# A pass that orders the finished instruction list of an encoder layer by due times

## The chip, the cores and the metric

The kernel runs on one core of a Trainium2 chip. A core has a matrix engine (TensorE, "PE" in the profile; its weight loads are "PEld"), a vector engine (VectorE, "DVE"), a scalar engine (ScalarE, "ACT"), a general engine (GpSimd, "POOL") and a sync engine (SyncE, "SP"). Here SP issues all the transfers between the chip's main memory (HBM) and the on-chip memory (SBUF). Each engine works through its own list of instructions in order and waits for the others by semaphores. Results of TensorE go to eight PSUM banks, from which VectorE and ScalarE take them.

The metric is the device time of one execution in microseconds (us); less is better.

## The reference

One layer over 2048 tokens of width 1024, in float32, and a final normalisation:

```python
xn = rms_norm(x, mix_norm_g)
aq, ak, av, mq, mk, mv, mo, ipre, fpre, ga, gm = split(xn @ w_in)
att = chunk_band_attention(aq, ak, av, rel_bias)      # 8 heads of 64, chunks of 64, own + 8 before
q, k = silu(causal_depthwise_conv(concat(mq, mk)))    # width 4
hm = mlstm_chunkwise(q, k, mv, ipre + b_igate, fpre + b_fgate)   # 4 heads of 128
mlstm_out = sigmoid(mo) * rms_norm_by_head(hm)
y = sigmoid(ga) * (att @ w_att_proj) + sigmoid(gm) * (mlstm_out @ w_mlstm_proj)
x = x + y @ w_out
x = x + square(relu(rms_norm(x, ffn_norm_g) @ w_up)) @ w_down    # 4096 wide
return rms_norm(x, final_norm_g)
```

## The kernel before

The 2048 tokens are four blocks of 512 (`b` 0 to 3), two blocks make a span (`s` 0 and 1). Activations lie with features on the partitions and tokens along the free axis, so most matmuls move 512 columns.

**Two halves of each number.** Products are to have float32 accuracy. A float32 operand is split into a rounded part (type fp32r) and the rest. ScalarE makes the rounded part (`copy`), VectorE the rest (`tensor_sub`), and three matmuls are summed: high x high, high x low, low x high (`mm3`, lines 496 to 498). A weight tile of 128 x 1024 is loaded by SP into one of four buffers `wraw`, then split into one of three buffers `wsp` (`split_now`: line 435 on ScalarE, line 437 on VectorE). Activations are split in `split` (lines 1032 to 1039) into `r` tiles.

**Quads.** The large products use a two-by-two block scheme with seven products in place of eight (`quad`, line 579, and `quad_tok`, line 607). Sums of weight blocks are built either on the fly from four raw tiles (`quad_w`, line 454), or ahead of time by `sum_w` (line 404), which loads blocks into `ctx` tiles, adds them on VectorE and stores them in HBM (`wsum`). The four bank results of a quad are put together by `combine`: ScalarE copies the first product of a pair (line 1678), VectorE adds the second (line 1686), and the bank is free. Among the quads are both halves of the gate `ga` in both spans: `GATES` lists ga0, ga1, gm0, gm1 for span 0, and `IN_ORDER` has them for span 1. `down` adds the products of w_down into accumulators (line 2082), `after_out` those of w_out (line 1900).

**Chains beside the dense work.** Attention goes head by head: scores (line 1227) are reduced against the bias (1233), exponentiated on ScalarE (1242), scaled by the reciprocal of their sum (1244, 1246), transposed on PE (1258), split (1261, 1263) and multiplied with the values (1196). The mLSTM goes head by head in four chunks: transposed keys are scaled (1494, 1498), then three matmuls per chunk (1519 to 1521), and the state `cst` is updated on VectorE (1524) before the next chunk. Outputs of both (`mix`) go to HBM and are loaded back for the projections (`take_u1`, lines 2000 and 1032).

**What sets the order.** Python generators, one per strand of work, ask for buffers, banks and engine time; `Flow` runs them against its own clock of each engine and so writes all instructions in one list. Chain matmuls are put `SLACK` = 800 ns behind the moment at which `Flow` thinks they are ready. Buffers and banks are fixed at this point. The framework's scheduler then takes this list in order of priority, and on each engine brings an instruction forward where it finds it ready before earlier ones, by its own estimates. For example the memset of `hist` (line 317), written behind the loading of the gate weights, runs 0.86 us after the start. So the order on the engines is the scheduler's, with the list as its priority.

The last step of the program's build is in `Layer.build`:

```python
fl.spawn(self.late(), 0)
fl.spawn(self.dense(), 5)
fl.run()
```

Of the kernel before, what the change touches and what calls it, by code (L numbers as in the profile page):

```python
# [15 lines left out]


# [1 line left out]

# [49 lines left out]
class Event:  # L69
    def __init__(self):  # L70
        self.at = None
# [23 lines left out]
class Flow:  # L95
# [22 lines left out]
    def set(self, ev):  # L118
        ev.at = self.now
# [53 lines left out]
    def run(self):  # L173
        while self.ready or self.blocked:
            moved = True
            while moved:
                moved = False
                for th in sorted(self.blocked, key=lambda x: (x.prio, x.n)):
                    ok, value = self._grant(th)
                    if ok:  # L180
                        self.blocked.remove(th)
                        self.now = th.at
                        self._step(th, value)
                        moved = True
            if not self.ready and not self.blocked:
                break
            if not self.ready:
                raise RuntimeError("no thread can go on")
            best = None
            for th in self.ready:  # L190
                t, frm = th.at
                for e in th.req[0].split("|"):
                    prio = th.prio
                    if e[-1] == "!":
                        e, prio = e[:-1], -1
                    start = t + self.LAT[frm].get(e, 0.0)
                    if e == "pe" and th.prio < 5:
                        start += self.SLACK
                    key = (max(self.clock[e], start), prio, th.n)
                    if best is None or key < best[0]:  # L200
                        best = (key, th, e)
            (start, _, _), th, e = best
            self.ready.remove(th)
            end = start + th.req[1]
            self.clock[e] = end
            if len(th.req) > 2:
                end += th.req[2]
            th.at = self.now = (end, e)
            self._step(th, e)
# [10 lines left out]
def dve2_ns(n):  # L220
    return 70 + 0.55 * n

class Layer:
# [648 lines left out]
    def operands(self):  # L874
        return [[None] * 4 for _ in range(7)], [[Event() for _ in range(4)] for _ in range(7)]
# [1335 lines left out]
    def build(self):  # L2211
        fl, nc = self.fl, self.nc
        E = lambda n: [Event() for _ in range(n)]
        self.vdram = [nc.dram_tensor(f"vspill{b}", (NT, P, D), F32R, kind="Internal") for b in range(NB)]
        f32d = lambda name, *shape: nc.dram_tensor(name, shape, F32, kind="Internal")
        self.td = [f32d(f"wsum{q}", 4, P, 1024) for q in range(N_Q + 2)]
        self.x2d = [f32d(f"x2_{b}", KT, P, T) for b in range(NB)]
        self.xnd = [f32d(f"xn{b}", KT, P, T) for b in range(2)]
        far = lambda name, *shape: {b: f32d(f"{name}{b}", *shape) for b in range(NB)}
        self.projd, self.proj_ev = f32d("proj", 2, KT, P, T), [E(KT), E(KT)]  # L2220
        self.mvfar = far("mvfar", NT, P, 512)
        self.qfar, self.kfar = far("qfar", 4, 2, P, T), far("kfar", 4, 2, P, T)
        self.mfar, self.gd = far("mfar", 3 * MH, P, T), far("gate", 2, KT, P, T)
        self.mixd = far("mix", 8, P, T)
        self.mix_kept = {b: [E(4 if i < 4 else 1) for i in range(8)] for b in range(NB)}
        self.ypd = [f32d(f"yp{b}", KT, P, T) for b in range(NB)]
        self.fin = [f32d(f"fin{h}", 4, P, T) for h in range(2)]
        self.ud = f32d("u", 4, 7, 4, P, T)
        self.wi = 0
        self.y3 = [{}, {}]  # L2230
        self.wtile = {}
        self.wev, self.wgot = collections.defaultdict(Event), collections.defaultdict(Event)
        self.td_ev = {q: E(2) for q in (*range(N_G, N_G + N_O + N_USUM), *range(N_Q - N_F, N_Q + 2))}
        self.t_ev = [[E(4) for _ in range(7)] for _ in range(NS)]
        self.xn_kept = [E(KT) for _ in range(2)]
        self.x_sent, self.w_sent = E(KT), E(KT // 2)
        self.last_ev, self.ev_late, self.ev_r, self.ev_gain, self.ev_const = (Event() for _ in range(5))
        self.u_ev = [[[E(4) for _ in range(7)] for _ in range(4)] for _ in range(NS)]
        self.v_ev, self.mv_ev = ({b: E(n) for b in range(NB)} for n in (2 * NT, NT))
        self.q_ev, self.k_ev, self.m_ev, self.g_ev = (collections.defaultdict(Event) for _ in range(4))  # L2240
        self.hist_ev = [E(2 * MH) for _ in range(NB)]
        self.yp_ev = [E(KT) for _ in range(NB)]
        jh = lambda: {(j, h): Event() for j in range(KT) for h in range(2)}
        self.acc = [{} for _ in range(NS)]
        self.acc_ev, self.acc_done, self.res_ev = [jh(), jh()], [jh(), jh()], [jh(), jh()]
        self.blk = []
        for b in range(NB):
            self.blk.append(dict(
                xs=[], xg=[], vs={}, xs_ev=Event(), xn=E(KT), xs_done=E(KT), x2=E(KT), v_slots=Event(), v_ev=E(NT), v_spilt=E(NT),
                kq_ev=E(AH), q_ev=E(AH), k_ev=E(AH), k_spilt=E(AH), kq_all=Event(), head_done=E(AH),  # L2250
                gates=Event(), mv_slots=Event(), mv_ev=E(NT), ctx={}, mvh={}, ctx_ev=E(MH), qk_ev=E(2 * MH), og_ev=E(MH),
                mix=[None] * 8, mix_ev=E(8), ga={}, ga_ev=E(8), xs_free=Event(), x_room=E(KT), mid=Event(), vo={}, vn={}, vp_ev=E(4), mvh_ev=E(MH), gf=Event(), rec_slots={}, heads_left=[2] * 4))
        fl.spawn(self.setup(), 0)
        fl.spawn(self.norm_in(0), 0)
        fl.spawn(self.loader(), 0)
        fl.spawn(self.late(), 0)
        fl.spawn(self.dense(), 5)
        fl.run()

# [81 lines left out]
```

## Time and profile before

| | |
|---|---|
| time, median of 3 runs | 2855.98 us (2854.34 to 2863.55) |
| the profiled execution | 2858.04 us, its span 2856.3 us |
| granted TensorE clock, mean | 0.997 |
| instructions | 39412 |
| TensorE, matmuls | 2801.4 us, 98% of the span |
| VectorE | 2014.5 us, 71% |
| ScalarE | 1526.5 us, 53% |
| GpSimd | 48.7 us, 2% |
| transfers | 662 MB, 232 GB/s on the mean |

A row of a group reads: line, engine, operation, tile written <- tiles read, shapes, count | busy us, mean ns of one | idle us of the engine just before them, and what ended that. A row of the waits reads: engine, tile and line that waited <- what it waited for: us in total, times, longest us. A row of the timeline reads: start us, length us, engine, line, operation, count, and in brackets the idle time before it and what ended it. A row of the chain that ended last has start us, us, and what it was. The busy time of TensorE is a union of records that overlap: one of 512 columns is 390 ns long in the records, and the next starts some 227 ns after it.

### The profile page before, as it was taken

The numbers are of one execution on the slowest core, as the hardware profiler recorded it, in microseconds if no ns is written. First come the engines' busy times: TensorE is split into PE (matmuls) and PEld (weight loads), VectorE is DVE, ScalarE is ACT, GpSimd is POOL, SyncE is SP. The second block draws the span as 40 slices with busy tenths as digits, with TensorE's granted clock in tenths as the row PEclk, the third lists the DMA queues.
The fourth block names the chain that finished last, engine by engine and source line by source line (L and its number), as shares of the span: only waits on it lengthen the run. The fifth ranks groups of instructions, "written<-read, shape, count | busy, mean of one in ns | idle before, by whom it ended". The sixth has DMA issues, their size and how long they took to land.

```text
span 2856.3 us, 39412 instructions
## 1 busy us (share of the span) xinstructions
PE 2801.4 (98%) x13528; PEld 2334.4 (82%) x13528; DVE 2014.5 (71%) x3743; ACT 1526.5 (53%) x2641; POOL 48.7 (2%) x100
## 2 busy tenths in 40 slices
PE   8999999999999999999999999999999999999998
PEld 7888887887878888878878888888888788888887
DVE  6695797667896866876666778789787744455565
ACT  4564576544344535574555565566535655554444
POOL 0010001000000000000000000000000000000000
PEclk9999999999999999999999999999999999999999
DMA  7867757768756678578877986787676655576563
GB/s 255 263 219 242 232 164 250 241 216 285 253 189 202 210 264 267 188 248 305 292 280 255 275 248 193 238 244 243 228 262 227 210 199 195 195 237 212 188 225 134
DMA packets 317736, 662.41 MB, mean 232 GB/s; under 512 B 35552, under 2 KB 62304, under 8 KB 317536
## 3 DMA queue, kind: packets, MB, share of 16 engines
q1 hardware_dynamic: 317536, 659.90, 70.7%
q8 instruction: 106, 1.74, 0.2%
q14 instruction: 94, 0.77, 0.1%
HBM read 462.63 MB, written 197.13 MB: 231 GB/s over the span
## 4 chain that ended last, share of the span: by engine, by line
PE 72%; DVE 11%; DMA 10%; ACT 3%; issue 3%; SPq 1%; POOL 0%; POOLq 0%; DVEq 0%; ACTq 0%
PE bank L579 31%; PE bank L496 11%; PE bank L497 10%; PE bank L498 10%; DVE wsp L437 2%; PE bank L607 2%; DMA wsum<-ctx 2%; PE bank L1196 2%; PE bank L1227 2%; PE bank L1258 1%; DMA ctx<-in_wf 1%; ACT wsp L435 1%; DVE r L1037 1%; DVE ctx L1857 1%; DVE ctx L1686 1%
## 5 line engine op out<-in xcount | busy, mean ns | idle before, releaser
L579 PE MATMUL bank<-r,wsp 128*128 128x512 f32 x5544 | 1268.4, 390 | 17.5 <-DVE ctx L1686 13.5
L579 PEld LDWEIGHTS bank<-r,wsp 128*128 128x128 f32 x5544 | 1039.3, 188 | 240.8 <-DVE ctx L1686 15.8
L437 DVE TENSOR_TENSOR wsp<-wraw,wsp 128x1024 fp32r<-128x1024 f32 x459 | 560.9, 1222 | 345.6 <-ACT wsp L435 332.7
L435 ACT CAST wsp<-wraw 128x1024 fp32r<-128x1024 f32 x459 | 482.0, 1050 | 463.4 <-PE bank L579 195.6
L496 PE MATMUL bank<-r,wsp 128*128 128x512 f32 x1472 | 590.8, 401 | 0.9 <-DVE scs L1233 0.4
L498 PE MATMUL bank<-r,wsp 128*128 128x512 f32 x1472 | 575.5, 391 | 0.0
L497 PE MATMUL bank<-r,wsp 128*128 128x512 f32 x1472 | 575.4, 391 | 0.0
L498 PEld LDWEIGHTS bank<-r,wsp 128*128 128x128 f32 x1472 | 276.6, 188 | 59.9
L496 PEld LDWEIGHTS bank<-r,wsp 128*128 128x128 f32 x1472 | 277.2, 188 | 49.8 <-DVE r L1263 1.2
L497 PEld LDWEIGHTS bank<-r,wsp 128*128 128x128 f32 x1472 | 277.6, 189 | 47.0
L1037 DVE TENSOR_TENSOR r<-r 128x512 fp32r<-128x512 f32 x264 | 176.5, 687 | 50.1 <-ACT r L1032 49.2
L1032 ACT CAST r<-r 128x512 fp32r<-128x512 f32 x264 | 160.0, 624 | 84.1 <-DMA r<-u 60.4
L1686 DVE TENSOR_TENSOR ctx<-bank,ctx 128x512 f32<-128x512 f32 x186 | 127.0, 687 | 78.9 <-PE bank L579 78.8
L1678 ACT COPY ctx<-bank 128x512 f32<-128x512 f32 x186 | 108.1, 582 | 68.5 <-PE bank L579 60.7
L1242 ACT ACTIVATE sc<-sc,scs 128x640 f32<-128x640 f32 (+4 forms) x128 | 98.0, 766 | 82.4 <-DVE scs L1239 73.7
L404 DVE TENSOR_TENSOR ctx<-ctx,ctx 128x512 f32<-128x512 f32 x112 | 76.7, 689 | 72.5 <-DMA ctx<-in_wf 40.9
L2016 ACT ACTIVATE ctx<-ctx 128x512 f32<-128x512 f32 x96 | 60.6, 631 | 111.3 <-DVE ctx L1686 111.3
L1233 DVE CUSTOM_DVE_ANT_0 sc<-bank,bias 128x320 f32<-128x320 f32 (+3 forms) x240 | 104.7, 461 | 13.2 <-PE bank L1227 12.6
L1196 PEld LDWEIGHTS bank<-r,r 128*128 128x128 f32 x672 | 98.0, 189 | 15.7 <-DVE r L1263 5.6
L1196 PE MATMUL bank<-r,r 128*128 128x256 f32 (+1 forms) x672 | 106.9, 280 | 4.0 <-DVE r L1263 3.3
L1263 DVE TENSOR_TENSOR r<-bank,r 128x512 fp32r<-128x512 f32 (+1 forms) x168 | 96.3, 594 | 13.0 <-ACT r L1261 12.1
L454 DVE TENSOR_TENSOR wraw<-wraw,wraw 128x1024 f32<-128x1024 f32 x76 | 92.6, 1220 | 2.0 <-DMA wraw<-in_wf 0.9
(247 smaller groups left out, 2775.7 us busy)
## 6 DMA issues: line engine op xcount, KB each, us to landing
wraw<-in_wf SPq DMA_DIRECT2D x178, 512.0 KB, 4.3
wraw<-wsum SPq DMA_DIRECT2D x136, 512.0 KB, 4.0
r<-u SPq DMA_DIRECT2D x224, 256.0 KB, 4.2
wraw<-in_w SPq DMA_DIRECT2D x88, 512.0 KB, 4.4
u<-ctx SPq DMA_DIRECT2D x128, 256.0 KB, 2.7
ctx<-in_wf SPq DMA_DIRECT2D x112, 256.0 KB, 4.0
wsum<-ctx SPq DMA_DIRECT2D x112, 256.0 KB, 3.6
u<-tmp SPq DMA_DIRECT2D x96, 256.0 KB, 2.8
```

Source lines behind the costliest of these rows:

```text
L435: nc.scalar.copy(w[:, 0], raw)
L437: nc.vector.tensor_sub(w[:, 1], raw, w[:, 0].bitcast(F32))
L496: mm(ps, lh, rh, start=first, stop=False)
L497: mm(ps, lh, rl, start=False, stop=False)
L498: mm(ps, ll, rh, start=False, stop=last)
L579: mm(ps, wv[:, x, k, n], a[:, y], start=new and k == 0 and x == y == 0, stop=k == 3 and x == 1, skip_group_check=True)
L1032: self.nc.scalar.copy(dst[:, 0], src)
L1037: self.nc.vector.tensor_sub(dst[:, 1], src, dst[:, 0].bitcast(F32))
L1196: nc.tensor.matmul(bk[:, c0:c0 + w], st, sl[:, x, o:o + w], start=n == 0, stop=n == total - 1)
L1233: nc.vector.tensor_tensor_reduce(out=e[:, x * w:x * w + w], in0=bks[x][:, :w], in1=br[:, j0 + x * w:j0 + x * w + w], op0=ALU.add, op1=ALU. ...
L1678: nc.scalar.copy(t[:, o:o + 512], ps)
L1686: nc.vector.tensor_add(t[:, o:o + 512], ps, t[:, o:o + 512])
```

## The change

`Layer.build` gets one more line at its end, `Order(self.tc).run()`, and a new class `Order` of some 145 lines. No instruction is added, removed or altered, and no buffer changes. The pass

- takes the finished list and prices each instruction by engine, shape and operands (`cost`, `transfer`);
- finds from the operands which instruction must follow which (`graph`): a read after a write, a write after either, and for a PSUM bank any two uses;
- gives each a due time (`due`): matmuls stand back to back in the list's order, and every other instruction is due so much ahead of the earliest of those that need it, as its own duration, a hand-over (`lag`) and, for a DMA, 2500 ns more ask for;
- plays all engines (`run`): at each step the engine that can go on first takes, on TensorE, the ripe instruction that is earliest in the list, and on the other engines and SP's queue the ripe one with the earliest due time. Ripe is an instruction whose inputs are there by the model and, other than on TensorE, have been for a margin (600 ns after TensorE, 100 ns after the others, 2500 ns after a transfer); if none is ripe, the one that will be ripe first is taken;
- adds edges (`NoSync`: they order, and wait for nothing) from each instruction to the next one of its engine in this order, so that the scheduler has no choice left.

```diff
+class Order:
+    MARGIN = dict(PE=600.0, Activation=100.0, DVE=100.0, Pool=100.0, SP=2500.0)
+    WAKE = dict(PE=43.0, DVE=23.0, Activation=23.0, Pool=69.0, SP=16.0)
+    REACH, LAND, FAR = 1400.0, 1100.0, 2500.0
...
+    def cost(self, i, e):
+        ins, outs = self.operands(i.ins), self.operands(i.outs)
+        n = max(self.count(a) for a in ins + outs)
+        bank = any(a.tensor.name.startswith("bank") for a in ins + outs)
+        if e == "PE":
+            return max(110.0, 13.7 + self.count(outs[0]) / 2.4)
+        if e == "SP":
+            return 365.0
+        if e == "Activation":
+            return (75 if bank else 93) + 0.84 * n + (190 if len(outs) > 1 else 0)
+        if e == "Pool":
+            return 1200.0 if n <= 8 else 80 + 1.27 * n
+        if n <= 4:
+            return 155.0
+        two = sum(self.count(a) > 4 for a in ins) > 1
+        return 60 + (1.13 if two or bank else 0.66) * n + (80 if len(outs) > 1 else 0)
+
+    def transfer(self, i):
+        a, b = self.operands((i.outs[0], i.ins[0]))
+        rows = min(list(x.ap)[0][1] for x in (a, b))
+        t = self.count(a) * list(a.ap)[0][1] * 0.0099
+        return max(60.0, t * (1.45 if 32 < rows <= 64 else 1.0))
...
+    def lag(self, j, k):
+        e, to = self.eng[j], self.eng[k]
+        if e == to != "SP":
+            return 0.0
+        t = self.WAKE[to] + (0.0 if e == "SP" else 13.0)
+        return t + (0.0 if e != "PE" else 175.0 if self.dur[j] >= 140.0 else 130.0)
+
+    def due(self):
+        n, t = len(self.ins), 0.0
+        due = [None] * n
+        for k in range(n):
+            if self.eng[k] == "PE":
+                due[k] = t
+                t += self.dur[k]
+        for k in range(n - 1, -1, -1):
+            d = t + 8000.0 if due[k] is None else due[k]
+            less = self.dur[k] + (self.FAR if self.eng[k] == "SP" else 0.0)
+            for j in self.succ[k]:
+                d = min(d, due[j] - less - self.lag(k, j))
+            due[k] = d
+        return due
+
+    def run(self):
...
+        for _ in range(n):
+            t, e = min((clock[e] if ripe[e] else max(clock[e], soon[e][0][0]), e)
+                       for e in self.WAKE if ripe[e] or soon[e])
+            while soon[e] and soon[e][0][0] <= t:
+                k = heapq.heappop(soon[e])[2]
+                heapq.heappush(ripe[e], (k if e == "PE" else due[k], k))
+            k = heapq.heappop(ripe[e])[1]
+            order[e].append(self.ins[k])
+            start = max(clock[e], at[k])
+            clock[e] = end = start + self.dur[k]
+            if e == "SP":
+                queue = max(queue, start + self.REACH) + self.transfer(self.ins[k])
+                end = queue + self.LAND
+            for j in self.succ[k]:
+                to = self.eng[j]
+                r = end + self.lag(k, j)
+                at[j] = max(at[j], r)
+                safe[j] = max(safe[j], r + (self.MARGIN[e] if to != "PE" and (to != e or e == "SP") else 0.0))
+                left[j] -= 1
+                if not left[j]:
+                    heapq.heappush(soon[to], (safe[j], due[j], j))
+        for o in order.values():
+            for a, b in zip(o, o[1:]):
+                self.tc.add_manual_dep(b, a.name, mybir.DependencyInfo(
+                    mybir.DependencyClass.NoSync, mybir.DependencyReason.DATA), reason="order")
...
         fl.run()
+        Order(self.tc).run()
```

More of the change, by code (lines that the diff above doesn't have):

```diff
@@ L18 @@
 import collections
+import heapq
 import concourse.bass as bass
@@ L221, in dve2_ns, with __init__, operands, count @@
     return 70 + 0.55 * n
+class Order:
+    MARGIN = dict(PE=600.0, Activation=100.0, DVE=100.0, Pool=100.0, SP=2500.0)
+    WAKE = dict(PE=43.0, DVE=23.0, Activation=23.0, Pool=69.0, SP=16.0)
+    REACH, LAND, FAR = 1400.0, 1100.0, 2500.0
+    def __init__(self, tc):
+        self.tc = tc
+        name = lambda i: str(i.engine).split(".")[-1]
+        self.ins = [i for i in tc.nc.cur_bb.bb.instructions if name(i) in self.WAKE and (i.ins or i.outs)]
+        self.eng = [name(i) for i in self.ins]
+        self.dur = [self.cost(i, e) for i, e in zip(self.ins, self.eng)]
+        self.graph()
+    @staticmethod
+    def operands(xs):
+        return [x.bass_ap for x in xs if hasattr(x, "bass_ap")]
+    @staticmethod
+    def count(a):
+        n = 1
+        for _, c in list(a.ap)[1:]:
+            n *= c
+        return n
+    @staticmethod
+    def region(a):
+        t, pat = a.tensor, [tuple(p) for p in a.ap]
+        if t.name.startswith("bank"):
+            return t.name, 0, 1, 0, 1
+        p0, p1, lo = 0, 1, a.offset
+        if type(t).__name__ == "Tile":
+            step = 1
+            for d in t.shape[1:]:
+                step *= d
+            p0, lo = divmod(a.offset, step)
+            p1, pat = p0 + pat[0][1], pat[1:]
+        hi = lo + sum(s * (c - 1) for s, c in pat if s > 0)
+        lo += sum(s * (c - 1) for s, c in pat if s < 0)
+        return t.name, p0, p1, lo, hi + 1
+    def cost(self, i, e):
[19 more added lines that the diff above has]
+        return max(60.0, t * (1.45 if 32 < rows <= 64 else 1.0))
+    def graph(self):
+        seen = collections.defaultdict(list)
+        self.succ, self.left = [[] for _ in self.ins], []
+        for k, i in enumerate(self.ins):
+            before = set()
+            for write, ops in ((False, i.ins), (True, i.outs)):
+                for a in self.operands(ops):
+                    t, p0, p1, f0, f1 = self.region(a)
+                    own = write or t.startswith("bank")
+                    keep = []
+                    for r in seen[t]:
+                        q0, q1, g0, g1, w, j = r
+                        if j != k and q0 < p1 and p0 < q1 and g0 < f1 and f0 < g1 and (own or w):
+                            before.add(j)
+                            if own and p0 <= q0 and q1 <= p1 and f0 <= g0 and g1 <= f1:
+                                continue
+                        keep.append(r)
+                    keep.append((p0, p1, f0, f1, own, k))
+                    seen[t] = keep
+            self.left.append(len(before))
+            for j in sorted(before):
+                self.succ[j].append(k)
+    def lag(self, j, k):
[19 more added lines that the diff above has]
+    def run(self):
+        due, n = self.due(), len(self.ins)
+        at, safe, left = [0.0] * n, [0.0] * n, self.left
+        clock = dict.fromkeys(self.WAKE, 0.0)
+        soon = {e: [] for e in self.WAKE}
+        ripe = {e: [] for e in self.WAKE}
+        order = {e: [] for e in self.WAKE}
+        queue = 0.0
+        for k in range(n):
+            if not left[k]:
+                heapq.heappush(soon[self.eng[k]], (0.0, due[k], k))
+        for _ in range(n):
[23 more added lines that the diff above has]
+                    mybir.DependencyClass.NoSync, mybir.DependencyReason.DATA), reason="order")
```

## The prediction

> **What bounds the kernel now.** I read the page's head first (span, busy time by engine), then the windows, then PE's waits, then the timeline around the longest of them.
>
> ```profile
> span 2856.3 us, 39412 instructions
> PE 2801.4 (98%) x13528; PEld 2334.4 (82%) x13528; DVE 2014.5 (71%) x3743; ACT 1526.5 (53%) x2641; POOL 48.7 (2%) x100
> L579 PE MATMUL bank<-r,wsp 128*128 128x512 f32 x5544 | 1268.4, 390 | 17.5 <-DVE ctx L1686 13.5
> ...
> 2348.06 181.05 PE bank L579 x798
> ...
> 2500.00:2571.00 71.00, 71.00 (x315) 58.80 (x314) 37.45 (x46) 38.34 (x56) 0.00 (x0) 1.00 0.70 236
> 2785.00:2857.00 72.00, 62.50 (x324) 52.52 (x322) 37.47 (x54) 32.02 (x47) 2.35 (x2) 0.95 0.38 132
> ...
> PE bank L579 <- DVE ctx L1686: 13.5, 11, 3.0
> PE bank L496 <- ACT wsp L435: 7.5, 1, 7.5
> PE bank L1519 <- ACT wsp L435: 5.5, 2, 4.4
> PE bank L1196 <- DVE r L1263: 3.3, 5, 1.0
> PE bank L1519 <- DVE tmp L1569: 2.9, 3, 1.5
> PE bank L579 <- DVE ctx L1900: 2.8, 1, 2.8
> ```
>
> TensorE is the bound: 2801.4 of 2856.3 us. In its best stretch 798 matmuls of 512 columns take 181.05 us, 226.9 ns each, and a window there (columns: window, its length, busy PE, PEld, DVE, ACT, POOL, clock, DMA share, GB/s) is full. The change adds and removes no matmul, so only time in which PE is not fed can be won: 2856.3 - 2801.4 = 54.9 us. Of that 7.5 are before the first matmul (the one wait of L496) and 8.8 lie in the last window (71.3 us of it belong to the span, 62.5 are busy). The first loads and the last normalisation keep those. **38.6 us** are left in the middle. They are not spread thin: eleven waits for L1686, two for L435 and a few more.
>
> The busy time hides something too. 5544 matmuls of L579 at 226.9 ns would be 1257.9 us, and their busy time is 1268.4: 10.5 us of short delays that the overlapped records cover.
>
> The two longest waits of the middle show what they are made of:
>
> ```profile
> 463.88 0.60 PE L1494 MATMUL bank<-const,r 128*128 128x128 f32 x4
> 466.53 2.01 ACT L1032 CAST r<-r 128x512 fp32r<-128x512 f32 x3 [3.43 <-DMA r<-mix]
> 468.45 0.88 ACT L1498 ACTIVATE ctx<-bank,g_ex 128x128 f32<-128x128 f32 x3
> 469.94 1.07 ACT L435 CAST wsp<-wraw 128x1024 fp32r<-128x1024 f32 x1
> 471.85 0.55 PE L1519 MATMUL bank<-r,ctx 128*128 128x129 f32 x1 [4.41 <-ACT wsp L435]
> ...
> 1471.50 1.42 DVE L404 TENSOR_TENSOR ctx<-ctx,ctx 128x512 f32<-128x512 f32 x2 [4.52 <-DMA ctx<-in_wf]
> 1472.84 0.68 DVE L1686 TENSOR_TENSOR ctx<-bank,ctx 128x512 f32<-128x512 f32 x1
> 1475.46 1.22 DVE L454 TENSOR_TENSOR wraw<-wraw,wraw 128x1024 f32<-128x1024 f32 x1
> 1476.60 0.68 DVE L1686 TENSOR_TENSOR ctx<-bank,ctx 128x512 f32<-128x512 f32 x1
> 1477.34 1.74 PE L579 MATMUL bank<-r,wsp 128*128 128x512 f32 x4 [2.98 <-DVE ctx L1686]
> ...
> 1477.30:1481.30 4.00, 3.96 (x10) 3.13 (x11) 3.50 (x4) 3.36 (x5) 0.00 (x0) 0.57 0.82 328
> 471.80:479.80 8.00, 7.96 (x35) 7.31 (x36) 5.73 (x12) 4.58 (x14) 0.00 (x0) 0.63 0.76 260
> 2216.80:2226.80 10.00, 9.97 (x44) 8.28 (x45) 9.96 (x15) 7.31 (x12) 0.00 (x0) 1.00 0.73 250
> ```
>
> At 463.88 PE transposes a key tile and ScalarE only has to scale it (L1498). But L1032 stands ahead of L1498 in ScalarE's order and waits 3.43 us for a load of mix, which the projection needs far later; PE stands 4.41 us. At 1467 VectorE waits 4.52 us for a weight block that L404 is to sum, for tiles wanted much later, while two finished banks wait for L1686 behind it; PE stands 2.98 us. Neither engine is short of time. Work that isn't urgent stands ahead of work that is, and waits for a DMA there. The windows right behind these two gaps show a clock of 0.63 over 8 us and 0.57 over 4 us: 8.0 x 0.37 + 4.0 x 0.43 = **4.7 us** more. Behind the 2.8 us wait for L1900, which ends at 2216.8, the clock is 1.00.
>
> The Trainium skill (TensorE: Matmul & The Clock Gate, "Why this matters for your kernels") says to leave no idle gap above about 3 us between bursts, or the clock falls to half. The trace agrees for the gaps of 4.41 and 2.98 us. By that rule alone only these two gaps would cost clock.
>
> **The change part by part.** The word "quads" costs nothing: ga0 and ga1 of both spans are quads in the kernel before, and the diff doesn't touch them. The edges join instructions of one engine, so they add no instruction and no wait between engines. What changes is the order on PE, ScalarE, VectorE, POOL and in SP's DMA queue, and with it which waits end last. I cost each by what its order does.
>
> *VectorE and ScalarE* (busy 71% and 53%, so there is room). `Order.run` takes on each the ripe instruction with the earliest due time, and what waits for a transfer counts as ripe only 2500 ns after its modelled landing, unless nothing else is ripe. So L1032 and L404 in the two places above go behind L1498 and L1686, whose due times hang on a matmul close by. What is late next is a VectorE that is simply full for some us; I leave an eighth of the 38.6 us for that. Won: 38.6 x 7/8 = 33.8, and the 4.7 us of clock with the gaps that cause them: 38.5 us. Of the 10.5 hidden us I count none and keep them for the low end.
>
> *SP's queue*. Every DMA gets a fixed place, with a due time 2500 ns ahead of its own need:
>
> ```profile
> L437 DVE TENSOR_TENSOR wsp<-wraw,wsp 128x1024 fp32r<-128x1024 f32 x459 | 560.9, 1222 | 345.6 <-ACT wsp L435 332.7
> ...
> SPq L417 <- DVE wsp L437: 480.8, 193, 8.3
> ...
> wraw<-in_wf SPq DMA_DIRECT2D x178, 512.0 KB, 4.3
> wraw<-wsum SPq DMA_DIRECT2D x136, 512.0 KB, 4.0
> r<-u SPq DMA_DIRECT2D x224, 256.0 KB, 4.2
> ```
>
> SP stands 480.8 us now behind weight loads whose raw buffer isn't free, with stores and loads queued behind it. In the pass a load takes its place when its buffer is modelled free, so this should shrink; it gives PE nothing beyond the waits counted. The pass prices a 512 KB load at 1400 + 1298 + 1100 = 3.8 us and a 256 KB one at 1400 + 649 + 1100 = 3.1 us, against measured 4.0 to 4.3 and 4.2. The 2.5 us margin covers that, cost taken 0. Bounds: with the cover gone, 0.5 us for each late weight tile; a tile that lands early gains nothing.
>
> *PE*. PE takes the first instruction of program order that is ripe, and PE's inputs get no margin. So a chain instruction goes to PE at the very moment at which the pass thinks it ready. Where the pass prices a step too low, PE stands for the difference:
>
> ```profile
> L1242 ACT ACTIVATE sc<-sc,scs 128x640 f32<-128x640 f32 x96 | 80.1, 834 | 64.2 <-DVE scs L1239 63.6 <-DVE ms L1377 0.3
> L1242 ACT ACTIVATION_READ_ACCUMULATOR sc<-sc,scs 128x1 f32 x128 | 24.6, 192 | 0.0
> ...
> L1246 DVE TENSOR_SCALAR sc<-sc,scs 128x640 f32<-128x640 f32 x96 | 52.6, 549 | 1.4
> L1524 DVE SCALAR_TENSOR_TENSOR cst<-cst,g_ex,bank 128x129 f32<-128x129 f32 x64 | 22.1, 346 | 17.2 <-PE bank L1521 12.0 <-ACT tmp L1567 4.7
> ```
>
> The softmax chain: exp is priced at 93 + 0.84 x 640 + 190 = 821 ns and takes 834 + 192 = 1026; the scaling L1246 at 60 + 0.66 x 640 = 482 and takes 549. 272 ns short, for 64 units (128 softmaxes, two to a unit): at most 17.4 us. The state update L1524 is priced at 60 + 1.13 x 129 = 206 and takes 346; three of four steps of 16 heads feed the next matmul: 48 x 0.14 = 6.7 us at most. Together 0 to 24.1 us. Most chain steps have dense matmuls to stand behind, and waits of this kind (L1196, L1519 for L1569) are 6.2 us now. I take a quarter, 6.0 us. A gain through a price that is too high is bounded by the 10.5 hidden us.
>
> *POOL* is 2% busy: 0. *Start and end*: the same loads and chain, ordered by due time; 0, and I put plus or minus 4 us (half of 7.5 or 8.8) on it for the range.
>
> **The sum.** The profiled execution took 2858.04 us, 1.7 more than its span, and stands 2.1 above the median of 2855.98. 2858.0 - 38.5 + 6.0 = 2825.5, and on the median's footing **2823 us**. All 43.3 us and 8.8 of the hidden ones won (10.5 less the 1.7 of clock already counted), and no new waits: 2858.0 - 52.1 - 2.1 = 2804; with the 4 us of start or end, 2800.
>
> **The rivals.**
> *Half way.* PE pays the whole 24.1 us for chains priced too low: 2858.0 - 38.5 + 24.1 - 2.1 = 2841. For it: PE's missing margin and the four rows above. Against it: the program's order already puts chain matmuls 800 ns behind their modelled readiness, and the pass doesn't bring them forward while earlier ones are ripe.
> *Slower: the fixed SP order.* A DMA whose buffer frees later than modelled holds all later ones, loads for PE among them, and no other order is possible any more. 459 weight tiles (row L437) pass through four raw buffers. The net 32.5 us are gone once these tiles come late by 71 ns on the mean. If one in five (92) makes PE wait 0.6 us, 55 us are added: 2823 + 55 = 2878. For it: the 480.8 us of row L417, and prices 0.2 to 1.1 us under the measured landings. Against it: in the full window at 2500 us PE runs on these loads without a wait.
> The Trainium skill speaks for this rival: the spec table of TensorE: Matmul & The Clock Gate calls the queues of ScalarE and VectorE strict FIFO, so nothing passes an instruction that waits. The trace agrees, L1498 behind L1032 is the case. By that rule a fixed order is as good as its times, and no better.
> *No change.* The scheduler's own order could come out the same, or the gain lie in waits that move: 2856. Against it: the two places above need another order to go away, and edges force one.
>
> **How the numbers follow.** Forecast 0.58, half way 0.21, slower 0.15, no change 0.06. A difference under 0.3% (8.6 us) can't be told from none here. 2823 and 2841 are beyond that: faster 0.79; same 0.06; slower 0.15. The range begins at 2798, just under the 2800 of full success. It takes in 2841 and 2856 and ends at 2868, which leaves out most of the slower case. Within the forecast alone I expect 2804 to 2836.
>
> **What would show it.** Right: PE's waits for L1686 and for L435 in the middle fall from 19 us to under 5, no window's clock under 0.98 between 60 and 2780 us, L404 and L1032 still wait for DMAs but no PE wait follows, and L417's share of SP's waits falls. PE's busy time stays at 2790 to 2801 us. Half way: PE's waits name L1246, L1524, L1263 in many pieces under 0.3 us. Slower: PE's waits name L437 or a load, SP's longest waits grow beyond 8.3 us. Wrong altogether if PE's busy time itself rises, because another order of matmuls costs more at each change between chain and dense work; I hold the number of such changes to be about the same.

## The result, and the profile after

The changed kernel takes 2825.11 us (median of 4 runs, 2820.53 to 2828.0) against 2855.97 us for the kernel before: ratio 0.9885, 95% interval 0.9863 to 0.9908. It is 30.9 us faster; 2823 us was forecast. In a later comparison the same kernel came to 2822.95 us, ratio 0.9888 (0.9875 to 0.9901).

The profiled execution took 2823.55 us. All line numbers are 148 higher than before, since the new class stands ahead: line 579 is now 727, 1686 is 1834, 435 is 583. In kernels that order only some engines they are 149 higher.

First the page's head and its largest group, then PE's whole list of waits longer than 1 us, then windows (columns as in the prediction):

```profile
span 2821.8 us, 39514 instructions
PE 2790.0 (99%) x13528; PEld 2333.5 (83%) x13528; DVE 2041.7 (72%) x3743; ACT 1528.1 (54%) x2641; POOL 51.3 (2%) x100
L727 PE MATMUL bank<-r,wsp 128*128 128x512 f32 x5544 | 1263.4, 390 | 1.6 <-ACT r L1182 1.2
```

```profile
PE bank L644 <- ACT r L1136: 6.1, 1, 6.1
PE bank L644 <- ACT r L1180: 3.4, 1, 3.4
PE bank L755 <- DVE ctx L1834: 2.0, 2, 1.6
PE bank L1406 <- DVE sc L1394: 1.9, 2, 1.4
PE bank L1642 <- DMA r<-mfar: 1.8, 2, 1.7
PE bank L1375 <- ACT tmp L2345: 1.7, 2, 1.4
PE bank L727 <- ACT r L1182: 1.2, 1, 1.2
```

```profile
60.00:2780.00 2720.00, 2703.07 (x13114) 2262.35 (x13113) 1980.92 (x3610) 1480.77 (x2571) 48.51 (x90) 1.00 0.71 236
1557.00:1563.00 6.00, 4.96 (x16) 3.73 (x17) 3.90 (x6) 3.33 (x5) 0.00 (x0) 0.72 1.04 402
2000.00:2050.00 50.00, 43.61 (x238) 35.92 (x237) 32.60 (x78) 24.78 (x45) 1.01 (x1) 0.97 0.75 253
```

The same long window of the kernel before:

```profile
60.00:2780.00 2720.00, 2681.47 (x12957) 2235.98 (x12956) 1934.58 (x3597) 1462.38 (x2545) 44.58 (x89) 1.00 0.72 234
```

PE's idle time in the middle fell from 38.5 to 16.9 us. The wait of 13.5 us for L1686, eleven times, is gone; at the other quad line (607, here 755) 2.4 us for it became 2.0. The largest group lost its idle time (17.5 to 1.6 us) and 5.0 us of busy time. The gain of 34.5 us in span, between the two profiled executions, is then 21.6 us of idle time in the middle, 11.4 us of busy time (2801.4 to 2790.0) and 1.4 us at the start (7.5 to 6.1 us before the first matmul). TensorE, VectorE, ScalarE and GpSimd have as many instructions as before; the 102 that the page counts more in all are not among them.

What ScalarE and VectorE wait for at transfers shrank too. Before, the largest of these waits were:

```profile
ACT r L1032 <- DMA r<-u: 60.4, 71, 3.0
DVE ctx L404 <- DMA ctx<-in_wf: 40.9, 21, 4.9
ACT r L1034 <- DMA r<-yp: 28.9, 11, 5.1
DVE ctx L404 <- DMA wsum<-ctx: 23.5, 13, 5.0
```

After, the same four:

```profile
ACT r L1180 <- DMA r<-u: 50.8, 48, 7.0
DVE ctx L552 <- DMA ctx<-in_wf: 12.7, 6, 3.2
ACT r L1182 <- DMA r<-yp: 8.1, 5, 3.4
DVE ctx L552 <- DMA wsum<-ctx: 3.4, 2, 1.9
```

Together 153.7 us before and 75.0 after. This sum goes with the gain here, but doesn't measure it: a run below has a smaller sum than the kernel before, and is slower. Of the 16.9 us left on PE, 9.7 are one gap at 1557 us and the stretch from 2000 to 2050 us.

### The profile page after: what moved, and what is told of

Read it like the earlier page. It is cut to its first block, busy times and chain, and to the rows that moved or that the text cites. A ratio compares the mean times of both kernels' runs of the same rounds, so it can differ in the third digit from the quotient of the medians.

```text
span 2821.8 us, 39514 instructions
## 1 busy us (share of the span) xinstructions
PE 2790.0 (99%) x13528; PEld 2333.5 (83%) x13528; DVE 2041.7 (72%) x3743; ACT 1528.1 (54%) x2641; POOL 51.3 (2%) x100
## 4 chain that ended last, share of the span: by engine, by line
PE 93%; DMA 3%; DVE 2%; ACT 1%; issue 1%; SPq 0%; POOL 0%; POOLq 0%; DVEq 0%; ACTq 0%
PE bank L727 44%; PE bank L644 12%; PE bank L645 12%; PE bank L646 12%; PE bank L1344 3%; PE bank L1375 2%; PE bank L1406 2%; PE bank L755 2%; DVE wsp L585 1%; PE bank L1667 0%; DMA wsum<-ctx 0%; PE bank L1668 0%; PE bank L1669 0%; DMA wraw<-in_w 0%; PE bank L1653 0%
## 5 line engine op out<-in xcount | busy, mean ns | idle before, releaser
L1834 DVE TENSOR_TENSOR ctx<-bank,ctx 128x512 f32<-128x512 f32 x186 | 126.9, 687 | 102.3 <-PE bank L727 102.1
L1180 ACT CAST r<-r 128x512 fp32r<-128x512 f32 x264 | 158.0, 622 | 61.6 <-DMA r<-u 50.8
L1409 ACT CAST r<-bank 128x512 fp32r<-128x512 f32 (+1 forms) x168 | 81.2, 515 | 35.9 <-PE bank L1406 31.9
```

Of the source, the lines that this page charges most:

```text
L1180: self.nc.scalar.copy(dst[:, 0], src)
L1834: nc.vector.tensor_add(t[:, o:o + 512], ps, t[:, o:o + 512])
```

## The experiments

The theory of the prediction, A: the gain comes from the order on VectorE and ScalarE, where work that isn't urgent stood ahead of urgent work. Rivals: B, it comes from SP's queue; C, from PE's own order. Times are medians; ratios are to the kernel before, measured in the same comparison (2853.7, 2855.02 and 2855.05 us in the three sets).

### One engine's order at a time

The loop that adds the edges runs over some engines only:

```diff
-        for o in order.values():
+        for e in ('DVE', 'Activation'):
+            o = order[e]
             for a, b in zip(o, o[1:]):
```

and with `('SP',)` and `('PE',)` in the two others.

> Edges on VectorE and ScalarE alone; PE, POOL and SP's queue stay with the scheduler. Theory A (the gain of 31 us comes from the order on VectorE and ScalarE, where work that isn't urgent stood ahead of urgent work): 2825 to 2835 us. Theory B (the gain comes from SP's queue, loads that no longer stand behind others): over 2848. Theory C (the gain comes from PE's own order): over 2848.

> Edges on SP's queue alone. Theory A: within 8 us of the kernel before (2848 to 2864), and PE's waits still name L1686's line (here 148 lines further down). Theory B: 2825 to 2838.

> Edges on PE alone. Theory A: within 8 us of the kernel before (2848 to 2864); PE's short delays under its overlapped records may fall, its waits stay at some 38 us in the middle. Theory C: 2825 to 2838.

Measured: VectorE and ScalarE alone 2890.57 us, ratio 1.0127 (1.0106 to 1.0147): **slower** by 37 us. SP alone 2845.47 us, 0.9972 (0.9961 to 0.9982): a quarter of the gain. PE alone 2880.61 us, 1.0096 (1.0081 to 1.0111): slower by 27 us. SP's and PE's times lie outside every range that was set for them. Theory A falls in this form, and so do B and C: none of the three gives the gain by itself. Two make the kernel slower, and the order of VectorE and ScalarE costs more than the whole change wins. What PE's order alone loses stays open.

With SP's order alone PE already waits less for VectorE at the quads (L728 is L579 of the kernel before, L1835 its L1686):

```profile
PE bank L728 <- DVE ctx L1835: 3.8, 5, 1.1
```

```profile
60.00:2780.00 2720.00, 2694.39 (x13010) 2247.15 (x13009) 1941.36 (x3595) 1469.11 (x2550) 45.04 (x89) 1.00 0.70 235
```

The 13.5 us of the kernel before are 3.8, and PE's idle time in the middle is 25.6 us in place of 38.5. (These two profiled executions lie 13.0 us apart, the medians 8.2.) So the wait that the prediction put down to VectorE's order hung on SP's order too.

In the timeline of the kernel with VectorE and ScalarE ordered, the longest wait shows why:

```profile
102.86 0.58 ACT L1410 CAST r<-bank 128x512 fp32r<-128x512 f32 x1 [1.87 <-PE bank L1407]
122.04 0.63 ACT L1050 ACTIVATE ctx<-ctx 128x512 f32<-128x512 f32 x1 [18.60 <-DMA ctx<-in_xt]
122.69 0.37 ACT L1355 COPY tmp<-bank 64x256 f32<-64x256 f32 x1
123.08 0.48 ACT L1410 CAST r<-bank 128x384 fp32r<-128x384 f32 x1
...
117.20 0.59 SPq L1048 DMA_DIRECT2D ctx<-in_xt  x1
...
123.62 0.58 PE L1345 MATMUL bank<-r,r 128*128 128x256 f32 x1 [10.28 <-ACT r L1410]
```

ScalarE's fixed order puts a square of the next block (L1050) ahead of an attention piece (L1410). In the pass's own play SP brings this load in time, with a margin of 2.5 us, unless nothing else was ripe for ScalarE. Here SP follows the scheduler, and issues this load at 117.20 only, behind loads of keys and queries. ScalarE stands 18.60 us and PE 10.28. The Trainium skill (TensorE: Matmul & The Clock Gate, the spec table) calls ScalarE's queue strict FIFO. The trace agrees: PE had nothing left to do from 113.34 (123.62 less 10.28), so the cast L1410 had its input by then, and it ran only behind L1050.

That gave theory D: the orders are worth something only when the queues agree, SP's above all with those of ScalarE and VectorE.

### All engines but one

The same edit with all engines but SP, and with all but PE.

> Edges on all engines but SP's queue. Theory D, formed on the runs with one or two engines ordered: the orders are worth something only when all queues agree, and above all SP's queue has to bring the loads in the order in which ScalarE and VectorE stand waiting for them. It expects 2865 to 2900 us, with long waits of ScalarE or VectorE for loads. Rival E: any three of the queues carry most of the gain, and the loss with two came from PE's order not fitting: 2825 to 2840.

> Edges on all engines but PE. Theory D in its strict form (every queue has to agree, PE too): over 2845 us. Theory D in its loose form (SP with ScalarE and VectorE have to agree; PE's order in the scheduler follows the same list and differs little): 2822 to 2835.

Without SP's edges: 2902.45 us, ratio 1.0165 (1.0141 to 1.019), the slowest of all. Without PE's edges: 2829.98 us, 0.9921 (0.9898 to 0.9944). So D holds in its loose form. Between the first of these and the changed kernel only SP's edges differ: SP's order is what makes the orders of the others right. PE's order, left to the scheduler, costs 0.36% by the two ratios (0.9921 and 0.9885), whose intervals overlap a little (from 0.9898 to 0.9908), so this cost isn't certain. Without SP's edges PE's largest waits are for bank sums and, longest at a time, behind chain instructions of ScalarE. Below them are two of ScalarE's waits for loads:

```profile
PE bank L728 <- DVE ctx L1835: 14.9, 6, 3.8
PE bank L1668 <- ACT ctx L1617: 12.0, 1, 12.0
PE bank L1345 <- ACT r L1410: 7.7, 1, 7.7
...
ACT ctx L1050 <- DMA ctx<-in_xt: 31.4, 4, 16.1
ACT r L1181 <- DMA r<-mix: 14.3, 4, 10.4
```

The four waits for transfers that were summed above are 93.0 us here, less than the 153.7 of the kernel before, and yet this kernel is 47 us slower. The sum doesn't tell the loss. What differs is that single waits are long: up to 16.1 us here, where none of those four was over 5.1.

### Due times, or only a common order

```diff
-                heapq.heappush(ripe[e], (k if e == "PE" else due[k], k))
+                heapq.heappush(ripe[e], (k, k))
```

> All engines get edges and the model's ripeness with its margins, but the ripe instruction that is earliest in the list is taken, in place of the one with the earliest due time. If the due times are what sorts urgent from not urgent: 2843 to 2865. If it is the margins and the calibrated durations that keep an engine from standing behind a transfer: 2820 to 2832.

2834.79 us, ratio 0.9935 (0.992 to 0.995). This lies between the two expectations. One order for all engines from one play, with the margins and with the list as priority, wins 0.65%; taking the earliest due time in place of the earliest in the list wins another 0.50%. Both parts are real: the interval doesn't reach 0.9908 or 1.

### The margin after a transfer

`MARGIN["SP"]` is 0 in place of 2500, and in a later run 5000:

```diff
-    MARGIN = dict(PE=600.0, Activation=100.0, DVE=100.0, Pool=100.0, SP=2500.0)
+    MARGIN = dict(PE=600.0, Activation=100.0, DVE=100.0, Pool=100.0, SP=0.0)
```

> The margin after a transfer is 0 in place of 2500 ns, so an instruction that waits for a load may be placed as soon as the model has the load landed, which is 0.2 to 1.1 us before it lands by the traces. If the margin is what keeps ScalarE and VectorE from standing behind a late load: 2840 to 2860. If the due times alone keep urgent work ahead: 2822 to 2832.

Without the margin 2888.03 us, ratio 1.0115 (1.009 to 1.014): slower than the kernel before, and by more than expected. The waits of PE and then of ScalarE and VectorE in this kernel:

```profile
PE bank L727 <- DVE ctx L1834: 21.7, 9, 4.8
...
ACT r L1180 <- DMA r<-u: 108.5, 85, 8.1
DVE ctx L552 <- DMA ctx<-in_wf: 43.0, 20, 6.0
ACT r L1182 <- DMA r<-yp: 28.5, 13, 5.1
DVE ctx L552 <- DMA wsum<-ctx: 21.2, 12, 5.3
```

The four waits for transfers are 201.2 us in place of 75.0, and PE waits 21.7 us for the bank sums of L1834, the wait that was 13.5 us in the kernel before. Only this one number differs, all queues come from one play, and the due times are the same. So it is the margin that keeps ScalarE and VectorE from standing behind a load, and this is the mechanism that the prediction read from the two gaps at 471 and 1477 us. Two things stay open. The margin also applies in SP's queue, to a load that reads what a store has written (SP's wait at line 547 for stores of weight sums is 23.4 us here and 11.0 in the changed kernel), so the run doesn't tell the queues apart. And list order without the margin was not run, so what a common order is worth with neither isn't known.

### What is left: chains priced too low, or late transfers

Hand-overs after ScalarE and VectorE priced longer, and VectorE's small instructions at what they take:

```diff
-        if n <= 4:
-            return 155.0
+        if n <= 64:
+            return 165.0
...
         t = self.WAKE[to] + (0.0 if e == "SP" else 13.0)
-        return t + (0.0 if e != "PE" else 175.0 if self.dur[j] >= 140.0 else 130.0)
+        t += dict(Activation=100.0, DVE=45.0).get(e, 0.0)
+        return t + (0.0 if e != "PE" else 175.0 if self.dur[j] >= 140.0 else 130.0)
```

> The hand-over after ScalarE is priced 100 ns longer and after VectorE 45 ns longer, and VectorE's instructions of up to 64 elements at 165 ns, which is what the trace of before shows for them. If chains priced too low are a cost of the changed kernel, as the prediction had it with 6.0 us: 2815 to 2822 us. If what is left is late transfers and full engines: 2823 to 2830.

2820.93 us, ratio 0.9884 (0.9866 to 0.9903), where the changed kernel has 0.9885 and 0.9888. The median lies in the first range, the ratio shows no difference. So no cost of these prices can be told; but the interval reaches 5 us to either side, and a cost of a few us isn't excluded. Nor does the edit price the chains in full: it adds 145 ns behind the two instructions of the softmax that the prediction found 272 ns short, and 45 behind the state update, found 140 short.

The last set ran the changed kernel again beside longer margins.

> The changed kernel as it is, once more, beside the next three on one chip: 2820 to 2829 us by the runs so far.

> The margin after a transfer is 5000 ns in place of 2500. The longest wait of PE left in the changed kernel is behind a load of u that takes 7.84 us to land, 4.7 more than the model gives it. If late transfers are still a cost there: 2812 to 2821 us. If 2500 ns covers nearly all of them, and a longer margin only pushes work back: 2822 to 2835.

> The margin of 5000 ns and the longer hand-over prices together. If both causes are real and separate: 2808 to 2817 us, under each of them alone. If one of them is nothing: as the better of the two.

> As the one before, and a transfer is due 5000 ns ahead of its need in place of 2500, so that loads also go out sooner. If the loads are late because they are issued late: 3 us or more under the one before. If their place in SP's queue is set by when buffers come free: the same within 3 us.

The changed kernel again: 2822.95 us, 0.9888 (0.9875 to 0.9901). With 5000 ns: 2841.9 us, 0.9953 (0.9941 to 0.9965), worse by 19 us. With 5000 ns and the new prices: 2827.71 us, 0.9905 (0.9893 to 0.9918). With transfers due 5000 ns ahead as well (`FAR`): 2832.73 us, 0.9926 (0.9913 to 0.9938). None of the three with 5000 ns came out as any of its expectations had it. The waits of the kernel with 5000 ns, PE's first and then the largest of ScalarE for transfers:

```profile
PE bank L644 <- ACT r L1136: 6.2, 1, 6.2
PE bank L1667 <- DMA r<-mvfar: 2.9, 1, 2.9
PE bank L727 <- ACT r L1182: 2.7, 2, 2.0
PE bank L1642 <- DMA r<-mfar: 2.7, 2, 2.0
...
PE bank L1375 <- DMA r<-kfar: 1.9, 1, 1.9
...
ACT wsp L583 <- DMA wraw<-in_wf: 8.2, 3, 6.5
ACT r L1180 <- DMA r<-u: 5.6, 5, 2.2
```

The long margin does what it says: the wait of ScalarE for loads of u falls from 50.8 to 5.6 us. PE is fed worse all the same: its idle time in the middle is 27.4 us, in place of 16.9. So the waits of ScalarE for transfers aren't a loss by themselves; of those left at 2500 ns, PE's list above has 4.6 us behind L1180 and L1182. That a longer margin pushes back work that was ready is the likely cause, but no run showed it by itself. One piece of it can be seen: PE's waits for loads that read back a stored tensor (`mvfar`, `mfar`, `kfar`) are 7.5 us here and 1.8 in the changed kernel, and the margin holds such a load back behind its store. Why the new prices win 14 us at 5000 ns and nothing at 2500 stays open too. Loads due sooner don't help: the median is 5 us higher than without, and the intervals overlap a little. No version is faster than the changed kernel by more than its runs scatter.

## Why the prediction was right

**Right: what bounds, and the size.** PE's feed was what could be won, and 32.5 us net of the recoverable 43.3 were forecast (33 on the footing of the medians); 30.9 came.

**Right: the mechanism in the two gaps.** Work behind a transfer stood ahead of urgent work. PE no longer waits at the two places, where L1498 and L1686 stood behind L1032 and L404, and taking the margin away brings the waits for L1686 back.

**The terms of the sum moved against each other, and that the total came within 2.1 us is luck.** Idle time in the middle: 33.8 less 6.0, so 27.8 us were forecast, 21.6 came. Busy time: only the 4.7 us of clock were counted, 11.4 came. Of the clock itself little was won, because the changed kernel has two slow stretches of its own (0.72 over 6 us at 1557, 0.58 over 4 us at 2040): 6.0 x 0.28 + 4.0 x 0.42 = 3.4 us are lost again, so some 1.3 us are won. The other 10 us are then, in the main, the short delays under the overlapped records, which the prediction kept for the low end; the busy time of the largest group alone fell from 10.5 us over its pace to 5.5, with 1.7 of clock in it before. The start gave 1.4 us where 0 was put.

**Of the signs, some came and some did not.** The 19 us of PE's waits in the middle for L1686 and L435 are gone (the 2.0 us left for L1686 are at a line that had 2.4), and PE's busy time of 2790.0 us lies at the end of its range. But the clock fell under 0.98 in two places, one PE wait does stand behind L1032's load (L1180 here), and SP's waits at L417 did not shrink.

**Not found: 6.0 us for chains priced too low.** PE's waits in the changed kernel name the scaling L1394 (L1246 before) with 1.9 us and the state update not at all, and longer prices changed nothing that can be told. Delays hidden under the records can't be told apart, so the true size stays open. Most of what is left is elsewhere: of the idle 16.9 us, 6.4 lie between 2000 and 2050 us, and one gap at 1557 us is behind a load. In the profile of the second comparison this gap is 1.8 us, so its length changes between executions.

The chain of waits has the load (start, length), the timeline what stands behind it:

```profile
1549.29 7.84 DMA r<-u
```

```profile
1557.15 1.93 ACT L1180 CAST r<-r 128x512 fp32r<-128x512 f32 x3 [7.04 <-DMA r<-u]
...
1557.82 0.51 PE L644 MATMUL bank<-r,wsp 128*128 128x512 f32 x1 [3.35 <-ACT r L1180]
```

**Wrong: "It gives PE nothing beyond the waits counted", of SP's queue.** The whole gain was put to VectorE and ScalarE. Their order alone loses 37 us, and all orders without SP's lose 47, while SP's order alone took most of the wait for L1686 (13.5 to 3.8 us). SP's order is half of a pair: the others are drawn up against its landings. It was also expected that SP stands less behind weight loads; L417's 480.8 us became 495.8 (L565 here):

```profile
SPq L565 <- DVE wsp L585: 495.8, 211, 7.4
```

**The slower rival was a real mechanism, not the outcome.** A fixed order that meets late transfers costs more than the change wins: with the margin at 0 the kernel is at 2888 us. That is near the 2878 worked out for it, but by another way: PE's largest wait there is for bank sums (L1834), not for weight tiles. Its deciding point was the cover of 2.5 us, not the four raw buffers. The half-way rival (2841) would have needed PE to pay 24.1 us for short prices, and nothing of that size shows.

## What to carry to other kernels

Fix the orders of the queues from one play of all of them: an order drawn up for one engine assumes when the others deliver, and alone it can cost more than the common order wins (37 us for VectorE and ScalarE here, against the 30.9 won). Above all, don't fix the order of the engines that wait for loads without that of the queue that brings them. This is one kernel; in it only SP's order won something alone. In an in-order queue, put what waits for a transfer late enough that a late landing stops nothing; here 2.5 us beyond the modelled landing was good, 0 and 5 us were both worse by 19 us or more. To find such a loss, look at what stands ahead of the instruction PE waited for, not at how busy its engine is.

## What the runs showed of the hardware

The clock after an idle gap of PE. In the changed kernel the gap of 3.35 us at 1557 us is followed by 0.72 over 6 us. In the kernel before, 4.41 us were followed by 0.63 over 8 us, 2.98 us by 0.57 over 4 us, and 2.8 us by 1.00. The Trainium skill (TensorE: Matmul & The Clock Gate, "Why this matters for your kernels") gives about 3 us as the longest gap without a drop; these four agree, and other places in the traces don't. With the margin of 5000 ns a gap of 1.89 us, with dense matmuls ahead of it, is followed by 0.63 over 4 us. In the changed kernel gaps of 1.37, 0.70 and 1.38 us between 2035 and 2040 us are followed by 0.58 over 4 us. The matmul behind the gap of 1.89 us, then the window of that kernel and the one of the changed kernel:

```profile
95.80 1.84 PE L1375 MATMUL bank<-r,r 128*128 128x128 f32 x12 [1.89 <-DMA r<-kfar]
...
96.00:100.00 4.00, 4.00 (x18) 3.42 (x18) 3.03 (x18) 2.44 (x6) 0.00 (x0) 0.63 1.06 327
...
2040.00:2044.00 4.00, 4.00 (x15) 3.35 (x15) 2.33 (x6) 2.62 (x5) 0.00 (x0) 0.58 0.93 333
```

So no bound on the length of a single gap comes out of these runs, and several short gaps close together can cost clock too.

A 256 KB load of u took 7.84 us to land, where the median of these loads is 4.1. While it was under way the core's DMA engines were busy throughout:

```profile
1549.29:1557.13 7.84, 5.18 (x23) 3.94 (x21) 3.74 (x9) 0.82 (x1) 1.32 (x1) 1.00 1.02 355
```

That is 355 GB/s at a DMA share of 1.02, against 236 at 0.71 from 60 to 2780 us. That this made it late is likely, and no run shows it by itself. The margin of 2500 ns on a modelled 3.1 us doesn't cover this load, and a margin that would cover it cost more than it won.
